# Newton's values partly in PSUM, held weight sums and an unsplit half of h in a two-layer fp32 step

## The chip, the cores and the metric

One Trainium2 chip, one of its cores. The metric is the device time of one launch in microseconds (us); smaller is better. TensorE does the matrix products; VectorE (DVE), ScalarE (ACT) and GpSimd (POOL) do the rest, each with its own in-order queue; SyncE (SP) issues nearly all DMAs, in a fixed list.

## The reference

One inference step of a two-layer model, all in fp32: 640 tokens (512 latent, 128 prompt), width 1024, feed-forward width 2816.

```python
every layer: x += 1/2 * gate1 * SwiGLU1(mod(rmsnorm(x)))
             x += gate2 * Mixer_l(mod(rmsnorm(x)))
             x += 1/2 * gate3 * SwiGLU2(mod(rmsnorm(x)))
mod(h) = h * (1 + scale) + shift

def rms_norm(x, g):
    y = x * rsqrt(mean(x * x, axis=-1) + EPS)
    return y * g
def swiglu(h, w_gate, w_up, w_down):
    return (silu(h @ w_gate) * (h @ w_up)) @ w_down
```

Layer 0's mixer is neighbourhood attention beside a bidirectional linear recurrence; layer 1's is a 2-D Fourier transform with a linear map. Shift, scale and gate come from a conditioning vector. Latent and prompt tokens have different ones.

## The kernel before, in words

The activations lie transposed: 1024 features are 8 chunks `c` of 128 partitions, and the 640 tokens are two halves `h` (0 and 1) of `HT` = 320 columns. An fp32 product is three products of rounded parts: each operand is split into a high and a low tile, and `mm3` (line 282) issues high by high, high by low and low by high. So each weight tile `st` that a DMA brings is split into `whi` (ACT, line 176) and `wlo` (DVE, line 181), and each chunk of the normed activations `h` into `hh` and `hl`.

The four SwiGLUs are the stages 0ffn1, 0ffn2, 1ffn1 and 1ffn2. Layer 0's mixer lies between the first two, layer 1's between the last two. Of the 22 blocks `f` of 128 hidden features the first two are made directly, from four weight tiles: the fill of `ffn_body`, a loop over half `h` and chunk number `n`, with product `j` inside. The rest are made by `quad`, a scheme of seven block products M1 to M7 in place of eight. It needs

- sums of weight blocks, made on POOL by `quad_b` (lines 226, 227) and `quad_c` (lines 231, 232) out of a gate tile and an up tile, and then split by ACT and DVE (`quad_a`, `quad_d`, `quad_e`, `quad_f`);
- the T factors, sums over the halves of h, tiles `T[0..3][k]`, `k` = 0 to 3. `t_sums` (line 528) makes them from the chunks `k` and `k+4` of both halves while half 1 is normed, in three steps; line 172 is the low part of their split.

`prep` takes the next steps of a list of weight work: it issues loads (`load`), the DVE low parts still due (`flush`) and one or more of the steps above. It is called at j = 3 of every `n`, so weight work and norm work stand in one order on each engine. A load is issued when a buffer `st` is free, and a split when a pair `whi`/`wlo` is free; both are kept in lists with a phase, and `buffers` adds some for one stage.

The norm of a half: the sums of squares come from TensorE into a bank `nst`; `rsqrt` (lines 415 to 422) takes the inverse root by three Newton steps of three small DVE operations (128 x 3 each), with `nv`, `nt` and `ns` in SBUF; the result is spread by a matmul to the bank `nbc`; then `norm_high` and `norm_low` make each chunk: line 473 multiplies x by `nbc`, ACT lines 479 and 481 apply scale and shift and take the high part, and line 495 makes the low part (on POOL for even chunks of half 0). For odd chunks of half 0 (`direct`) one DVE operation (line 469), one of ACT (line 471) and one of DVE (line 492) do the same. Tiles `y` rotate through three buffers. Half 0 of the next stage is normed inside the last product of the stage before, chunk by chunk after the update of x (line 381); half 1 inside the fill's h = 0 (start) and h = 1.

The scratch PSUM bank has room beside the few columns that `nst` uses. In `t_sums` half 0 is only there split, so the factors that need it take the high part, and then the low part in an operation of its own:

## Time and profile before

| | us |
|---|---|
| median of 3 runs (lowest, highest) | 2299.74 (2299.42, 2300.52) |
| profiled execution, its own time | 2300.82 |
| its span in the profile | 2299.0 |
| TensorE busy in the span | 2223.4 |
| DVE busy | 1550.3 |
| ACT busy | 990.1 |
| POOL busy | 953.6 |

The profiled execution's own time is 1.8 us longer than its span, and 1.1 us above the median. Stages by time in the span: 0ffn1 to about 515 us, layer 0's mixer to about 835, 0ffn2 to about 1305, 1ffn1 to about 1770, layer 1's mixer to about 1855, 1ffn2 to the end. In a timeline row the columns are: start, length of one group, engine, line, operation, output from inputs, shapes, count, and in square brackets the idle time of the engine ahead of it with what ended it. In a table of stretches each row is one stretch: its length, then each engine's busy time with its number of instructions, the granted TensorE clock as a share of the full one, the share of the DMA engines' time, and GB/s.

### The profile page before, as it was taken

The page shows a single profiled execution, that of the slowest core. Times are in us where ns is not written, and L with a number is a line of the kernel's source. Part 1 is how long each engine was busy: PE and PEld are TensorE (multiplying, and loading weights), DVE is VectorE, ACT ScalarE, POOL GpSimd, SP SyncE. Part 2 cuts the span into 40 slices and gives each one's busy share as a digit, 9 for nine tenths or more (in the row PEclk, how much of TensorE's full clock was granted, in tenths as well). Part 3 has the DMA queues.
Part 4 walks back from the last instruction along what each step waited for, and adds up shares of the span by engine and source line. Part 5 has one row for each costly group of instructions (what it writes and reads, how often), then busy time and mean ns, then how long its engine had stood idle before and what let it go on. Part 6 is the DMA issues. An engine that isn't in the chain of part 4 may idle for free.

```text
span 2299.0 us, 39900 instructions
## 1 busy us (share of the span) xinstructions
PE 2223.4 (97%) x15534; PEld 2111.4 (92%) x15534; DVE 1550.3 (67%) x2871; ACT 990.1 (43%) x1780; POOL 953.6 (41%) x856
## 2 busy tenths in 40 slices
PE   6899999999998899999999999999999989999999
PEld 5899999999995798999999989999999979999999
DVE  6676676666865368666666786666667786666665
ACT  4433333347765444333333453333335553333332
POOL 2544444440023235444444454444443645444441
PEclk9999999999999999999999999999999999999999
DMA  7333333321228424322332143332232322222221
GB/s 279 113 108 104 110 104 111 106 83 56 67 74 272 130 96 144 108 94 102 111 106 85 67 156 123 107 110 93 101 111 62 129 91 78 83 83 83 83 90 56
DMA packets 75317, 245.44 MB, mean 107 GB/s; under 512 B 8757, under 2 KB 12997, under 8 KB 75129
## 3 DMA queue, kind: packets, MB, share of 16 engines
q1 hardware_dynamic: 74168, 241.28, 31.0%
q8 instruction: 123, 2.02, 0.4%
q10 hardware_dynamic: 864, 1.38, 0.2%
q14 instruction: 66, 0.53, 0.1%
q0 software_dynamic: 96, 0.22, 0.0%
HBM read 239.71 MB, written 3.15 MB: 106 GB/s over the span
## 4 chain that ended last, share of the span: by engine, by line
PE 78%; DVE 12%; ACT 4%; issue 2%; POOL 2%; DMA 2%; DVEq 0%; SPq 0%; ACTq 0%; POOLq 0%
PE q L282 39%; PE pd L282 27%; PE pj L282 5%; DVE wlo L181 2%; PE ada L327 2%; DVE tl L172 1%; DMA st<-w_ada 1%; PE gt L1014 1%; PE pg L282 1%; PE pos L1549 1%; DVE x L381 1%; ACT hh L481 1%; DVE y L473 1%; DVE hl L495 0%; POOL u L825 0%
## 5 line engine op out<-in xcount | busy, mean ns | idle before, releaser
L181 DVE TENSOR_TENSOR wlo<-st,whi 128x1024 fp32r<-128x1024 f32 (+2 forms) x401 | 496.3, 1248 | 11.9 <-ACT whi L176 11.0
L176 ACT ACTIVATE whi<-st 128x1024 fp32r<-128x1024 f32 (+2 forms) x405 | 401.2, 992 | 235.2 <-POOL st L232 143.5
L282 PE MATMUL pd<-g,whi 128*128 128x320 f32 x1536 | 347.6, 311 | 2.7 <-DVE u L825 2.0
L381 DVE SCALAR_TENSOR_TENSOR x<-pd,mods,x 128x128 f32<-128x128 f32 (+2 forms) x696 | 265.1, 431 | 113.7 <-PE pd L282 113.5
L282 PE MATMUL q<-hh,wlo 128*128 128x320 f32 x960 | 297.0, 309 | 5.6 <-DVE wlo L181 5.6
L282 PE MATMUL q<-hh,whi 128*128 128x320 f32 x960 | 300.9, 313 | 0.6 <-DVE u L825 0.5
L282 PE MATMUL q<-th,whi 128*128 128x320 f32 x960 | 297.9, 310 | 3.0 <-DVE sg L825 3.0
L282 PE MATMUL q<-tl,whi 128*128 128x320 f32 x960 | 297.3, 310 | 0.7 <-POOL tl L172 0.7
L282 PE MATMUL q<-th,wlo 128*128 128x320 f32 x960 | 297.1, 310 | 0.0
L282 PE MATMUL q<-hl,whi 128*128 128x320 f32 x960 | 296.4, 309 | 0.0
L231 POOL TENSOR_TENSOR st<-sums,st 128x512 f32<-128x512 f32 x80 | 117.9, 1474 | 399.6 <-DVE wlo L181 362.2
L825 POOL TENSOR_TENSOR u<-u,u 128x320 f32<-128x320 f32 x80 | 107.4, 1343 | 402.0 <-DVE u L825 402.0
L282 PEld LDWEIGHTS pd<-g,whi 128*128 128x128 f32 x1536 | 257.6, 188 | 6.8 <-issue 2.9
L282 PE MATMUL pd<-hh,whi 128*128 128x320 f32 x768 | 238.7, 311 | 0.0
L282 PE MATMUL pd<-hl,whi 128*128 128x320 f32 x768 | 238.2, 310 | 0.0
L282 PE MATMUL pd<-g,wlo 128*128 128x320 f32 x768 | 238.1, 310 | 0.0
L282 PE MATMUL pd<-hh,wlo 128*128 128x320 f32 x768 | 237.2, 309 | 0.0
L826 ACT ACTIVATE sg<-sg 128x320 f32<-128x320 f32 x160 | 75.4, 471 | 284.2 <-DVE sg L825 284.2
L282 PEld LDWEIGHTS q<-hh,whi 128*128 128x128 f32 x960 | 180.4, 188 | 16.3 <-issue 8.6
L282 PEld LDWEIGHTS q<-th,whi 128*128 128x128 f32 x960 | 180.8, 188 | 6.3 <-issue 5.1
L282 PEld LDWEIGHTS q<-hh,wlo 128*128 128x128 f32 x960 | 180.2, 188 | 6.7 <-DVE wlo L181 6.7
L282 PEld LDWEIGHTS q<-tl,whi 128*128 128x128 f32 x960 | 181.0, 189 | 1.5 <-POOL tl L172 1.5
(327 smaller groups left out, 5006.9 us busy)
## 6 DMA issues: line engine op xcount, KB each, us to landing
st<-w_ada SPq DMA_DIRECT2D x144, 512.0 KB, 4.5
st<-ffn_gate SPq DMA_DIRECT2D x88, 512.0 KB, 3.5
st<-ffn_up SPq DMA_DIRECT2D x88, 512.0 KB, 3.6
st<-ffn_down SPq DMA_DIRECT2D x96, 384.0 KB, 3.0
st<-w_in SPq DMA_DIRECT2D x20, 512.0 KB, 3.5
st<-ffn_down SPq DMA_DIRECT2D x16, 512.0 KB, 3.5
st<-w_out_ab SPq DMA_DIRECT2D x8, 512.0 KB, 3.6
st<-w_out_c SPq DMA_DIRECT2D x8, 512.0 KB, 3.5
```

The lines of the kernel that those rows point to most:

```text
L172: (eng or self.nc.vector).tensor_tensor(out=lo, in0=src, in1=hi.bitcast(F32), op=ALU.subtract)
L176: self.nc.scalar.activation(out=hi, in_=src, func=AF.Copy)
L181: self.low.tensor_tensor(out=lo, in0=src, in1=hi.bitcast(F32), op=ALU.subtract)
L231: self.nc.gpsimd.tensor_tensor(out=s[:, 0:512], in0=it.s1, in1=s[:, 0:512], op=ALU.subtract)
L282: self.nc.tensor.matmul(out, lhsT=l, rhs=r, start=first and j == 0, stop=last and j == len(ops) - 1)
L327: nc.tensor.matmul(self.ada_ps[32 * j:32 * j + 32, 0:256], lhsT=self.s_sb[:, k, :], rhs=t[:, 256 * j:256 * j + 256], start=k == 0, stop=k ...
L381: self.nc.vector.scalar_tensor_tensor(out=self.x[h][c][:, sl], in0=ps[:, sl], scalar=gate[:, c, r:r + 1], in1=self.x[h][c][:, sl], op0=ALU ...
L473: nc.vector.tensor_tensor(out=y, in0=self.x[h][c], in1=r, op=ALU.mult)
L481: nc.scalar.activation(out=hi, in_=y, func=AF.Copy)
L825: tt = lambda e, o, a, b, op=ALU.add: e.tensor_tensor(out=o, in0=a, in1=b, op=op)
L826: cp = lambda o, p, fn=AF.Copy: nc.scalar.activation(out=o, in_=p, func=fn)
L1014: nc.tensor.matmul(g[:, s, 0:322], lhsT=wt[:, d, j, :], rhs=xc[:, 322 * s:322 * s + 322], start=True, stop=True)
```

## The change

1. In `rsqrt`, `v` and `t_` lie in columns 4 to 8 and 8 to 12 of the PSUM bank that holds the sums of squares, and the products are ordered so that each of the 11 operations has an operand there. Their number stays.
2. Where the four T factors' pool is made whole (ahead of 0ffn2, 1ffn1 and 1ffn2, not 0ffn1), it gets eight tiles `raw0`. Half 0 of the normed activations stays there unsplit; `t_sums` reads it, and drops two POOL operations for each `k`, 24 in all. `direct` is off there, so 12 odd chunks take lines 473, 479, 481 and 495.
3. 0ffn1 gets one more raw weight buffer and one more `whi`/`wlo` pair.
4. In the fill of 0ffn2 and 1ffn1, the first four `n` of h = 0 only load and flush. The weight steps that stood there (the sums of quad f = 2) come at n = 4 to 6.
5. Two small parameter loads go through ACT's queue and not POOL's, and the scratch space for POOL's DMA descriptors is set to 1024 bytes.

```diff
 def rsqrt(self, ps, n=3):
-        v, s, t_ = (self.t2.tile([P, 3], F32, tag=t, name=t)[:, :n] for t in ("nv", "ns", "nt"))
+        v, s, t_ = (x[:, :n] for x in (ps[:, 4:8], self.t2.tile([P, 3], F32, tag="ns", name="ns"), ps[:, 8:12]))
...
-            nc.vector.tensor_tensor(out=t_, in0=s, in1=s, op=ALU.mult)
-            nc.vector.scalar_tensor_tensor(out=t_, in0=t_, scalar=-0.5, in1=v, op0=ALU.mult, op1=ALU.mult)
+            nc.vector.tensor_tensor(out=t_, in0=v, in1=s, op=ALU.mult)
+            nc.vector.scalar_tensor_tensor(out=t_, in0=t_, scalar=-0.5, in1=s, op0=ALU.mult, op1=ALU.mult)
 def T_pool(self, ks=range(4)):
+        self.raw0 = [tp.tile([P, HT], F32, name=f"r{c}") for c in range(KD)] if len(ks) == 4 else None
 def norm_high(self, h, l, i, c, r, keep):
+        elif keep and not h and self.raw0:
+            y = self.raw0[c]
 def direct(self, l, i, h, c, keep):
-        return h == 0 and c % 2 == 1
+        return h == 0 and c % 2 == 1 and not (keep and self.raw0)
 def t_sums(self, k, b12, b22):
+        if self.raw0:
+            b11, b21 = self.raw0[k], self.raw0[k + 4]
...
-        tt(self.T_ENG[0], b12, b12, l11)
+        if not self.raw0:
+            tt(self.T_ENG[0], b12, b12, l11)
...
-        tt(nc.gpsimd, t4, t4, l21, ALU.add)
+        if not self.raw0:
+            tt(nc.gpsimd, t4, t4, l21, ALU.add)
 def ffn(...):
-            self.buffers(gp, ph, 3, 0)
+            self.buffers(gp, ph, *((4, 1) if ph == "0ffn1" else (3, 0)))
 def ffn_body(...):
-                    if j == 3:
+                    if j == 3 and h == 0 and n < 4 and (l, i) != (1, 2):
+                        self.flush()
+                        self.load()
+                    elif j == 3:
                         self.prep(self.n_use + 1, 1)
...
-            nc.gpsimd.dma_start(out=pk, in_=a["pk"])
+            nc.scalar.dma_start(out=pk, in_=a["pk"])
...
-    nc = _bacc.Bacc("TRN2", target_bir_lowering=False, num_devices=1)
+    nc = _bacc.Bacc("TRN2", target_bir_lowering=False, num_devices=1, dynamic_dma_scratch_size=1024)
```

The change moves instructions at three places. First, DVE at the start of 1ffn1, from the last chunk of half 0's norm to the Newton steps of half 1 (`st_`, `wlo_` and `whi_` are weight buffers by number, `hl_102` and `hh_101` chunk 7 of h, `r_7855` its unsplit tile). Before:

```order
L469 SCALAR_TENSOR_TENSOR y<-x_85,sc,nbc 128x320
L492 SCALAR_TENSOR_TENSOR hl_102<-y,mods,hh_101 128x320
L181 TENSOR_TENSOR wlo_76<-st_66,whi_75 128x1024
L181 TENSOR_TENSOR wlo_68<-st_65,whi_67 128x1024
L415 TENSOR_SCALAR nv<-nst 128x3
L417 TENSOR_SCALAR ns<-nv 128x3
L420 TENSOR_TENSOR nt<-ns 128x3
L421 SCALAR_TENSOR_TENSOR nt<-nt,nv 128x3
```

The same place in the change:

```order
L477 TENSOR_TENSOR r_7855<-x_85,nbc 128x320
L499 TENSOR_TENSOR hl_102<-r_7855,hh_101 128x320
L181 TENSOR_TENSOR wlo_74<-st_64,whi_73 128x1024
L415 TENSOR_SCALAR nst<-nst 128x3
L417 TENSOR_SCALAR ns<-nst 128x3
L420 TENSOR_TENSOR nst<-nst,ns 128x3
L421 SCALAR_TENSOR_TENSOR nst<-nst,ns 128x3
```

Of the two weight splits ahead of the Newton steps one is left. The other stands later on DVE, in the norm of half 1 (`b_13218` is chunk 0 of half 1, `pg` and `sg` belong to the SwiGLU of block 0); 0ffn2 has both moves too:

```order
L499 TENSOR_TENSOR hl_96<-y,hh_95 128x320
L534 TENSOR_TENSOR b_13218<-b_13218,r_7848 128x320
L181 TENSOR_TENSOR wlo_76<-st_66,whi_75 128x1024
L737 TENSOR_TENSOR sg<-sg,pg 128x320
L172 TENSOR_TENSOR g_13122<-sg,g_13121 128x320
```

Second, POOL at the start of 0ffn2, from the low parts of half 0 through the weight sums to the T factors of k = 0 and 1 (`t_` and `b_` are factors being made, `tl_` their low parts). Before:

```order
L495 TENSOR_TENSOR hl_100<-y,hh_99 128x320
L226 TENSOR_TENSOR sums<-st_65 128x512
L227 TENSOR_TENSOR st_65<-st_66,st_65 128x512
L231 TENSOR_TENSOR st_66<-sums,st_66 128x512
L232 TENSOR_TENSOR st_66<-st_66 128x512
L528 TENSOR_TENSOR t_8576<-y,b_8559 128x320
L528 TENSOR_TENSOR b_8559<-b_8559,hl_88 128x320
L528 TENSOR_TENSOR t_8638<-hh_95,y 128x320
L528 TENSOR_TENSOR t_8638<-t_8638,hl_96 128x320
L172 TENSOR_TENSOR tl_7870<-t_8576,th_7869 128x320
L528 TENSOR_TENSOR t_8656<-y,b_8570 128x320
```

In the change:

```order
L499 TENSOR_TENSOR hl_100<-r_7854,hh_99 128x320
L534 TENSOR_TENSOR t_8565<-y,b_8548 128x320
L226 TENSOR_TENSOR sums<-st_66 128x512
L227 TENSOR_TENSOR st_66<-st_64,st_66 128x512
L231 TENSOR_TENSOR st_64<-sums,st_64 128x512
L232 TENSOR_TENSOR st_64<-st_64 128x512
L534 TENSOR_TENSOR t_8632<-r_7852,y 128x320
L172 TENSOR_TENSOR tl_7873<-t_8565,th_7872 128x320
L534 TENSOR_TENSOR t_8649<-y,b_8559 128x320
```

The four sums go behind the first T operation, and each k has three POOL operations in place of five.

Third, DVE near the end of 0ffn1, where its last product updates x and half 0 is normed for the mixer (`x_86` is half 1 of x, `hl_90` chunk 1). Before:

```order
L473 TENSOR_TENSOR y<-x_85,nbc 128x320
L492 SCALAR_TENSOR_TENSOR hl_90<-y,mods,hh_89 128x320
L181 TENSOR_TENSOR wlo_68<-st_64,whi_67 128x1024
L381 SCALAR_TENSOR_TENSOR x_86<-pd,mods,x_86 128x192
L381 SCALAR_TENSOR_TENSOR x_86<-pd,mods,x_86 128x128
```

In the change:

```order
L477 TENSOR_TENSOR y<-x_85,nbc 128x320
L496 SCALAR_TENSOR_TENSOR hl_90<-y,mods,hh_89 128x320
L381 SCALAR_TENSOR_TENSOR x_86<-pd,mods,x_86 128x192
L381 SCALAR_TENSOR_TENSOR x_86<-pd,mods,x_86 128x128
```

One weight split of three among these updates has left the place; it now stands ahead of the earlier weight work, where the buffer pair added in 0ffn1 is free.

## The prediction, on record before the change was run

> **What bounds the kernel now.** I read the page's busy times first, then the table of stretches, then TensorE's timeline at the stretches that lose time, then DVE's and POOL's timelines there.

> ```profile
> PE 2223.4 (97%) x15534; PEld 2111.4 (92%) x15534; DVE 1550.3 (67%) x2871; ACT 990.1 (43%) x1780; POOL 953.6 (41%) x856
> ```

> TensorE bounds the kernel, and the change leaves its instructions alone. Only time that TensorE loses can be won. The table says where that is.

> ```profile
> 60.00:120.00 60.00, 52.32 (x370) 47.64 (x369) 40.27 (x68) 26.28 (x51) 30.60 (x26) 0.97 0.34 119
> 500.00:535.00 35.00, 30.41 (x199) 28.88 (x200) 30.07 (x76) 22.38 (x41) 12.53 (x30) 1.00 0.21 69
> 835.00:930.00 95.00, 88.27 (x605) 81.61 (x605) 78.95 (x134) 42.63 (x79) 51.15 (x45) 0.96 0.38 134
> 930.00:1270.00 340.00, 340.00 (x2360) 331.55 (x2359) 217.47 (x355) 131.38 (x218) 148.26 (x119) 1.00 0.30 100
> 1300.00:1400.00 100.00, 94.47 (x669) 86.20 (x668) 79.35 (x136) 43.77 (x83) 51.93 (x46) 0.98 0.40 138
> 1850.00:1912.00 62.00, 56.03 (x360) 51.90 (x361) 52.42 (x89) 32.12 (x65) 37.30 (x35) 0.94 0.25 85
> ```

> From 930 to 1270 TensorE has no gap: 340 us for 2360 matmuls, 0.144 us each. By that pitch the starts of the stages lose 60 - 370 x 0.144 = 6.7 us (0ffn1), 35 - 199 x 0.144 = 6.3 (its end), 7.9 (0ffn2), 3.7 (1ffn1) and 10.2 (1ffn2), some 35 us. The change works at these five places and nearly nowhere else. The losses are single waits of TensorE:

> ```profile
> 76.12 0.41 PE L282 MATMUL pg<-hh,whi 128*128 128x320 f32 x1 [4.44 <-ACT hh L481]
> 120.06 0.56 PE L282 MATMUL pd<-g,whi 128*128 128x320 f32 x2 [1.99 <-DVE u L825]
> 514.94 0.38 PE L282 MATMUL pj<-hh,whi 128*128 128x320 f32 x1 [2.54 <-ACT hh L471]
> 881.93 0.41 PE L282 MATMUL q<-hh,wlo 128*128 128x320 f32 x1 [1.65 <-DVE wlo L181]
> 898.58 0.39 PE L282 MATMUL q<-th,whi 128*128 128x320 f32 x1 [1.09 <-DVE sg L825]
> 1307.88 0.42 PE L282 MATMUL pg<-hh,wlo 128*128 128x320 f32 x1 [2.60 <-DVE wlo L181]
> 1881.65 0.41 PE L282 MATMUL pg<-hl,whi 128*128 128x320 f32 x1 [1.74 <-DVE hl L495]
> 1909.69 0.55 PE L282 MATMUL q<-th,whi 128*128 128x320 f32 x1 [1.88 <-DVE sg L825]
> ```

> and behind the longer ones, slices in which the granted clock is half:

> ```profile
> 121.20:124.60 3.40, 3.40 (x15) 3.40 (x14) 3.27 (x10) 2.40 (x3) 0.00 (x0) 0.50 0.56 212
> 1309.00:1312.40 3.40, 3.40 (x15) 3.40 (x14) 3.12 (x9) 0.00 (x0) 2.55 (x2) 0.50 0.93 335
> 1909.80:1913.20 3.40, 3.40 (x13) 3.40 (x14) 2.04 (x6) 1.86 (x4) 0.06 (x1) 0.51 0.47 161
> ```

> Such a slice does 13 to 15 matmuls where the dense pitch does 24. It costs (24 - 15) x 0.144 = 1.3 us by the count and 3.4 / 2 = 1.7 by the clock; I take 1.5. Slices stand behind the gaps of 1.99, 2.60 and 1.88 us; the gaps of 1.74 and 1.65 had none. So a gap that shrinks below about 1.8 us should win 1.5 us on top.

> **The change, part by part.**

> *Newton in PSUM.* In 0ffn2 the Newton steps of half 1 run while POOL makes weight sums:

> ```profile
> 842.69 0.15 DVE L415 TENSOR_SCALAR nv<-nst 128x3 f32<-128x3 f32 x1
> 842.87 1.05 DVE L417 TENSOR_SCALAR ns<-nv 128x3 int32<-128x3 int32 x1
> 848.47 0.16 DVE L422 SCALAR_TENSOR_TENSOR ns<-nt,ns 128x3 f32<-128x3 f32 x1
> 850.18 0.49 DVE L473 TENSOR_TENSOR b<-x,nbc 128x320 f32<-128x320 f32 x1 [0.75 <-PE nbc L453]
> 841.79 2.10 POOL L226 TENSOR_TENSOR sums<-st 128x512 f32<-128x512 f32 x1 [1.65 <-DMA st<-ffn_up]
> 887.36 0.47 DVE L729 TENSOR_TENSOR sg<-sg,pg 128x320 f32<-128x320 f32 x1
> 887.05 1.54 POOL L226 TENSOR_TENSOR sums<-st 128x512 f32<-128x512 f32 x1
> ```

> Line 417, all in SBUF, takes 1.05 us under POOL's line 226; the same kind takes 0.16 without it. Line 415, which reads PSUM, takes 0.15 under it, and line 729, which reads PSUM, 0.47 in the middle of another sum. So an operation with a PSUM operand does not wait for POOL. Four of the 11 operations are long here, about 4 x 0.9 = 3.6 us of DVE time. TensorE has the fill's h = 0 to do meanwhile, and waits only for the end of it: I count 0.7 us in 0ffn2 (the wait at nbc), and set the same in 1ffn2 against the longer ACT work below. A write to PSUM by a small DVE operation is nowhere in this trace; the bounds are 0.16 us (no cost) and 1.05 us (as bad as a delayed one), and I take 0.16, by the nearer row, line 415, which has one side in PSUM. With 11 x 0.9 us at the six norms on the path the upper bound would be 60 us, but most of that would be covered as the 3.6 us are now.

> [...]

> *Held sums.* In 1ffn1 half 0's first matmuls wait for weight splits that stand two in a row on DVE; one of the two splits a weight for the later quad:

> ```profile
> 1305.54 3.41 DVE L181 TENSOR_TENSOR wlo<-st,whi 128x1024 fp32r<-128x1024 f32 x2
> 860.20 0.89 POOL L528 TENSOR_TENSOR t<-hh,y 128x320 f32<-128x320 f32 x1 [5.20 <-DVE y L528]
> ```

> Without it, and without the four sums that slow DVE there, the gap of 2.60 shrinks by about half of 3.41, 1.7 us, and falls below 1.8: -1.7 - 1.5 = -3.2 us. The bounds are 0 (another wait takes its place) and -2.6 - 1.5 = -4.1. The held sums cost POOL 6.3 us (2.1 + 3 x 1.4, by the first and the 887.05 row's length) and land behind the first T operation, where POOL now idles 5.2 us; the remaining 1 us comes back from the dropped operations. If the cover is gone, the T factor of k = 0 is late by about 1 us.

> *Unsplit half 0.* The norm of half 1 sets the pace in the fill's h = 1:

> ```profile
> 865.24 0.47 DVE L473 TENSOR_TENSOR y<-x,nbc 128x320 f32<-128x320 f32 x1
> 869.36 1.16 DVE L495 TENSOR_TENSOR hl<-y,hh 128x320 fp32r<-128x320 f32 x1
> 872.34 0.47 DVE L473 TENSOR_TENSOR y<-x,nbc 128x320 f32<-128x320 f32 x1
> 868.27 1.02 POOL L528 TENSOR_TENSOR t<-t,hl 128x320 f32<-128x320 f32 x1
> 1303.68 0.56 ACT L471 ACTIVATE hh<-y,mods 128x320 fp32r<-128x320 f32 x1 [0.61 <-DVE y L469]
> 1855.65 1.07 DVE L417 TENSOR_SCALAR ns<-nv 128x3 int32<-128x3 int32 x1
> 1856.96 1.14 DVE L421 SCALAR_TENSOR_TENSOR nt<-nt,nv 128x3 f32<-128x3 f32 x1
> 1848.07 0.65 ACT L479 ACTIVATE y<-y,mods,sc 128x320 f32<-128x320 f32 x1 [5.60 <-DVE y L473]
> 1848.76 0.47 ACT L481 ACTIVATE hh<-y 128x320 fp32r<-128x320 f32 x1
> ```

> A pair of chunks takes 872.34 - 865.24 = 7.10 us of DVE; TensorE needs 24 matmuls x 0.144 = 3.5 us and the weight work between. Each of the dropped POOL operations lasts 1.0 us and stretches one DVE operation beside it by up to 1.16 - 0.48 = 0.7. Two fewer per pair give 1.4 us at most and I take 0.8. Over the two or three pairs that bind this closes the gap of 1.74 (1ffn2: -1.7) and half of 1.65 (0ffn2: -0.8); the T chain behind is one POOL operation shorter, which closes 1.09 (0ffn2: -1.0) and 1.0 of 1.88 (1ffn2: -1.0, and half a slice, -0.8). Against it ACT does 0.65 + 0.47 - 0.56 = 0.56 us more per odd chunk, 2.2 us per stage. In 0ffn2 and 1ffn1 this lies beside DVE's x updates; in 1ffn2 the norm of half 0 is on the path, and the 2.2 us are partly met by Newton, where the two long operations at 1855.65 and 1856.96 lose 1.9: +0.3 by the difference, and I take +0.8 since ACT's work comes first. DVE's part stays: two operations for two.

> *The extra buffers in 0ffn1.*

> ```profile
> 95.42 1.29 POOL L226 TENSOR_TENSOR sums<-st 128x512 f32<-128x512 f32 x1 [9.85 <-DMA st<-ffn_up]
> 72.76 1.54 DVE L473 TENSOR_TENSOR y<-x,acc 128x320 f32<-128x320 f32 x1
> 66.21 0.49 DVE L473 TENSOR_TENSOR b<-x,acc 128x320 f32<-128x320 f32 x1
> 511.27 1.90 DVE L181 TENSOR_TENSOR wlo<-st,whi 128x1024 fp32r<-128x1024 f32 x1
> ```

> POOL waits 9.85 us for a tile that no free buffer let in earlier. With one more it starts sooner, the chain of the first quads is earlier, and the gap of 1.99 with its slice goes: -3.5 us. But the sums move up beside the norm of half 1, where a DVE operation takes 1.54 for 0.49, and I add 1.5 to the gap of 4.44. Net -2.0; bounds +3 (two more stretched operations and no gap closed) and -5.6. At the stage's end one split fewer stands among the x updates, of 1.90 us; the wait of 2.54 loses 1.8, bounds 0 and -2.5.

> *The two parameter loads and the scratch space* lie at the very start. No row prices them; I set 0, and -0.5 to +0.5 as bounds, about one small operation (0.55) won on POOL's queue or lost on ACT's.

> **The sum.** 0ffn1 start -2.0, its end -1.8; 0ffn2 -0.7 - 0.8 - 1.0 and -0.7 for its smaller gaps = -3.2; 1ffn1 -3.2; 1ffn2 -1.7 - 1.8 + 0.8 = -2.7. Together -12.9. On the profiled execution 2300.8 - 12.9 = 2287.9; that execution stands 1.1 above the median, so I forecast **2287 us**. Less than 0.2%, 4.6 us either way, is about what a measurement cannot tell from no change.

> **The rivals.**

> *Half gains.* The waits move on to the next engine: in 1ffn1 the wait for wlo becomes one for its `whi`, and the 4.44 of 0ffn1 grows as much as the later gap shrinks. Then only the terms that a shorter queue gives outright remain, -1.8 at 0ffn1's end and -1.0 twice: 2296, within 0.2%. For it speaks that five engines meet at these places; against it that ACT is busy 43% and POOL 41%.

> *The slices stay.* The half clock may come at fixed moments behind any start of a stage. Then -1.5 twice and -0.8 are lost: 2291. The three slices behind gaps of 1.88 or more and none behind 1.74 speak against it. [...]

> *Slower.* The held sums and their split land in the T stretch of 0ffn2 and 1ffn1, which DVE paces. One split (1.9 stretched) and four sums, each stretching a DVE operation by 0.7, make 1.9 + 2.8 = 4.7 us per stage more on DVE; less 3 pairs x 0.8 won leaves +2.3, and a gap above 1.8 brings a slice of 1.5: +3.8 twice, with +3 in 0ffn1: 2310. It decides if DVE's pair stays at 7.1 us and the sums do not fit POOL's idle 5.2.

> *PSUM is dear.* If a small PSUM write costs as much as a delayed SBUF operation, 1.05, Newton grows by 7 x 0.9 = 6 us on DVE where 4 of 11 are long now, some 2 us of it seen at four of the starts: 2287 + 8 = 2295.

> **Chances.** The forecast 0.55, slices stay 0.15, half gains 0.13, PSUM dear 0.07, slower 0.10. The range holds the first three and PSUM's price on the upper side, to 2297; on the lower, the far ends of the terms (0ffn1 -5.6 and -2.5, 1ffn1 -4.1, and -6 and -5 for 0ffn2 and 1ffn2 if the pair wins 1.4 in place of 0.8 and their small gaps close) make -23, 2277. Faster by over 0.2% (under 2295): 0.76; within: 0.15; slower: 0.09.

> **What would show it.** Newton's operations all at 0.15 to 0.2 us beside POOL's sums; a pair at about 6.3 us; no gap of 1.7 or more at 881, 1307 and 1881; full clock behind them; POOL's wait of 9.85 gone and TensorE's wait near 76 at 4.4 to 6; x updates near 513 one split earlier. The prediction is wrong if the gaps reappear behind `sg`, `hl` or `hh` in the same stretches, or if the T stretch of 0ffn2 ends later than before, counted from the stage's start.

## The result, and the profile after

The change takes 2286.3 us (median of 6 runs, 2285.29 to 2291.68), the kernel before 2300.82 (median of 6, 2299.42 to 2302.80): ratio 0.994, 95% interval 0.9928 to 0.9952. That is 14.5 us less; 2287 was forecast, from terms that sum to 12.9 us less. The profiled execution has a span of 2283.8 us, 15.2 shorter than before's 2299.0. The direction and the total came out; the parts did not all come out, and one assumption behind the sum was wrong.

The page's busy times: the count of matmuls is the same, POOL has 26 operations fewer (the 24 of the T factors and two DMA issues) and ACT 12 more.

```profile
PE 2217.3 (97%) x15534; PEld 2104.6 (92%) x15534; DVE 1540.5 (67%) x2871; ACT 993.5 (44%) x1792; POOL 948.9 (42%) x830
```

The table of stretches, with the starts and ends moved to the same places of the program (the first row has the same times as before):

```profile
60.00:120.00 60.00, 54.92 (x396) 50.26 (x396) 46.30 (x81) 27.77 (x53) 31.77 (x26) 1.00 0.40 133
495.00:530.00 35.00, 31.16 (x205) 29.36 (x204) 29.25 (x80) 21.43 (x40) 12.67 (x30) 1.00 0.17 54
829.00:919.40 90.40, 85.42 (x605) 78.50 (x605) 73.20 (x134) 43.80 (x81) 43.64 (x36) 1.00 0.41 140
1290.50:1386.80 96.30, 93.01 (x667) 84.81 (x668) 74.74 (x136) 44.72 (x85) 44.78 (x37) 1.00 0.43 144
1836.80:1895.40 58.60, 53.98 (x362) 50.09 (x362) 46.55 (x87) 33.27 (x69) 30.44 (x26) 0.98 0.25 84
```

In 60 us TensorE does 396 matmuls for 370; the stretch of 605 matmuls in 0ffn2 takes 90.4 us for 95.0. The clock column stands at 1.00 in four of the five, where it had 0.97, 1.00, 0.96, 0.98 and 0.94.

Since both kernels issue the same 15534 matmuls in the same order, the start of each can be compared with the start of the same one before. By this the profiled executions, one launch each, differ as follows (good to a few tenths, since some records can be missing):

| place (time before) | measured, us | forecast |
|---|---|---|
| 0ffn1, start (0 to 128) | -5.8 | -2.0 (with the next row) |
| 0ffn1, middle (128 to 490) | +1.7 | |
| 0ffn1, end (490 to 535) | -0.9 | -1.8 |
| layer 0's mixer (535 to 830) | -0.9 | 0 |
| 0ffn2, start (830 to 930) | -4.5 | -3.2 |
| 930 to 1290 | +0.4 | 0 |
| 1ffn1, start (1290 to 1400) | -3.0 | -3.2 |
| 1400 to 1853 | -0.3 | 0 |
| 1ffn2, start (1853 to 1930) | -2.3 | -2.7 |
| 1930 to the end | +0.8 | 0 |

TensorE's waits of the change, from its timeline:

```profile
69.11 0.42 PE L282 MATMUL pg<-hh,whi 128*128 128x320 f32 x1 [1.59 <-ACT hh L485]
75.31 0.42 PE L282 MATMUL pg<-hh,whi 128*128 128x320 f32 x1 [2.35 <-ACT hh L485]
130.37 0.56 PE L282 MATMUL pd<-g,whi 128*128 128x320 f32 x2 [1.22 <-DVE x L381]
509.84 0.38 PE L282 MATMUL pj<-hh,whi 128*128 128x320 f32 x1 [1.63 <-ACT hh L475]
830.77 0.41 PE L282 MATMUL pg<-hh,wlo 128*128 128x320 f32 x1 [1.71 <-DVE wlo L181]
1297.13 0.41 PE L282 MATMUL pg<-hh,wlo 128*128 128x320 f32 x1 [1.05 <-DVE wlo L181]
1847.22 1.05 PE L455 MATMUL nbc<-dg,ones 128*128 128x128 f32 x6 [1.20 <-DVE dg L430]
1867.51 0.42 PE L282 MATMUL pg<-hl,whi 128*128 128x320 f32 x1 [0.86 <-DVE hl L499]
1878.05 0.42 PE L282 MATMUL q<-hh,wlo 128*128 128x320 f32 x1 [0.94 <-DVE wlo L181]
1893.85 0.39 PE L282 MATMUL q<-th,whi 128*128 128x320 f32 x1 [1.51 <-DVE sg L836]
```

One wait of before at these places, and the two half-clock slices behind it, do not stand in the prediction's lists:

```profile
837.03 0.41 PE L282 MATMUL pg<-hh,wlo 128*128 128x320 f32 x1 [1.90 <-DVE wlo L181]
838.00:844.80 6.80, 6.80 (x30) 6.80 (x29) 5.88 (x9) 2.57 (x5) 3.79 (x3) 0.50 0.55 172
```

4.44 became 2.35, 2.54 became 1.63, 1.90 became 1.71, 2.60 became 1.05, 1.74 became 0.86 and 1.88 (near 1909) 1.51; those near 120, 881 and 898 are under a microsecond. New are 1.59 us near 69, 1.22 near 130 and 1.20 at `nbc` in 1ffn2. So of the 2.1 us that the wait of 4.44 lost, 1.6 stand in the new wait ahead of it. The clock's slices behind the waits are gone in this launch; one is left in layer 0's mixer (at 768) and three in a row at the end of layer 1's:

```profile
831.00:834.40 3.40, 3.40 (x27) 3.40 (x27) 1.90 (x6) 3.27 (x7) 0.87 (x1) 1.00 0.50 159
1297.20:1300.60 3.40, 3.40 (x23) 3.40 (x24) 2.40 (x13) 0.00 (x0) 0.00 (x0) 1.00 0.69 234
1829.20:1832.60 3.40, 3.28 (x16) 3.22 (x16) 2.57 (x14) 0.00 (x0) 0.00 (x0) 0.50 0.01 2
```

Half of the time at half clock, summed over the span, is 17.2 us before and 7.2 in the change: 10 of the 15 us. The profiled launch of the change has the highest granted clock of its six (0.997; the others 0.992 to 0.996), and the launches of before in all experiments have 0.988 to 0.993. So part of these 10 us belongs to this launch.

### The profile page after: what moved, and what is told of

It reads as the page before. It is cut to its first block, busy times and chain, and to the rows that moved or that the text cites. A ratio compares the mean times of both kernels' runs of the same rounds, so it can differ in the third digit from the quotient of the medians.

```text
span 2283.8 us, 39869 instructions
## 1 busy us (share of the span) xinstructions
PE 2217.3 (97%) x15534; PEld 2104.6 (92%) x15534; DVE 1540.5 (67%) x2871; ACT 993.5 (44%) x1792; POOL 948.9 (42%) x830
## 4 chain that ended last, share of the span: by engine, by line
PE 78%; DVE 11%; ACT 5%; issue 2%; POOL 1%; DMA 1%; ACTq 0%; DVEq 0%; SPq 0%; POOLq 0%
PE q L282 40%; PE pd L282 26%; PE pj L282 5%; DVE wlo L181 2%; PE ada L327 2%; DVE tl L172 1%; DMA st<-w_ada 1%; DVE hl L499 1%; ACT hh L485 1%; PE gt L1025 1%; PE pos L1560 1%; DVE x L381 1%; ACT sx L1282 0%; DVE y L477 0%; ACT r L483 0%
## 5 line engine op out<-in xcount | busy, mean ns | idle before, releaser
L181 DVE TENSOR_TENSOR wlo<-st,whi 128x1024 fp32r<-128x1024 f32 (+2 forms) x401 | 499.8, 1257 | 16.2 <-ACT whi L176 15.6
L282 PE MATMUL pd<-g,whi 128*128 128x320 f32 x1536 | 347.6, 311 | 2.0 <-DVE x L381 1.9
L282 PE MATMUL q<-hh,whi 128*128 128x320 f32 x960 | 301.0, 314 | 1.0 <-DVE u L836 1.0
L282 PE MATMUL q<-hh,wlo 128*128 128x320 f32 x960 | 297.1, 310 | 2.9 <-DVE wlo L181 2.9
L282 PE MATMUL q<-th,whi 128*128 128x320 f32 x960 | 297.4, 310 | 2.2 <-DVE sg L836 2.2
L282 PE MATMUL q<-th,wlo 128*128 128x320 f32 x960 | 296.8, 309 | 0.0
L282 PE MATMUL q<-hl,whi 128*128 128x320 f32 x960 | 296.5, 309 | 0.0
L282 PE MATMUL q<-tl,whi 128*128 128x320 f32 x960 | 296.4, 309 | 0.0
L231 POOL TENSOR_TENSOR st<-sums,st 128x512 f32<-128x512 f32 x80 | 125.0, 1563 | 367.8 <-DVE wlo L181 353.8
L282 PEld LDWEIGHTS pd<-g,whi 128*128 128x128 f32 x1536 | 256.9, 188 | 6.9 <-issue 3.3
L282 PE MATMUL pd<-hh,whi 128*128 128x320 f32 x768 | 239.8, 312 | 0.0
L282 PE MATMUL pd<-hl,whi 128*128 128x320 f32 x768 | 238.5, 311 | 0.0
L282 PE MATMUL pd<-hh,wlo 128*128 128x320 f32 x768 | 238.2, 310 | 0.0
L282 PE MATMUL pd<-g,wlo 128*128 128x320 f32 x768 | 237.1, 309 | 0.0
L282 PEld LDWEIGHTS q<-hh,whi 128*128 128x128 f32 x960 | 180.4, 188 | 16.7 <-issue 9.9
L282 PEld LDWEIGHTS q<-th,whi 128*128 128x128 f32 x960 | 180.4, 188 | 5.6 <-issue 3.5
L282 PEld LDWEIGHTS q<-hh,wlo 128*128 128x128 f32 x960 | 180.3, 188 | 3.7 <-DVE wlo L181 3.7
L282 PEld LDWEIGHTS q<-th,wlo 128*128 128x128 f32 x960 | 180.7, 188 | 0.0
```

The lines of the kernel that those rows point to most:

```text
L181: self.low.tensor_tensor(out=lo, in0=src, in1=hi.bitcast(F32), op=ALU.subtract)
L231: self.nc.gpsimd.tensor_tensor(out=s[:, 0:512], in0=it.s1, in1=s[:, 0:512], op=ALU.subtract)
L282: self.nc.tensor.matmul(out, lhsT=l, rhs=r, start=first and j == 0, stop=last and j == len(ops) - 1)
```

## The experiments

The theory to test (A): each part shortens its own waits of TensorE, the half-clock slices go with the waits, and the parts add. The rival (B): the gain belongs to the clock alone, and the parts overlap. Part 5 (the parameter loads and the scratch space) was not run by itself; it is in the runs of the unsplit half alone and of the buffers alone. Ratios below are to the kernel before, on the same chip, with 95% intervals; 0.001 is 2.3 us.

### Each part alone

**Newton alone.** The diff is part 1 of the change, against before:

```diff
-        v, s, t_ = (self.t2.tile([P, 3], F32, tag=t, name=t)[:, :n] for t in ("nv", "ns", "nt"))
+        v, s, t_ = (x[:, :n] for x in (ps[:, 4:8], self.t2.tile([P, 3], F32, tag="ns", name="ns"), ps[:, 8:12]))
```

> Part 1 alone (Newton's v and t_ in PSUM), all else as before. Theory A (the parts add: each shortens its own waits of TensorE, and the half-clock slices go with the waits that it shortens): all 11 operations of a Newton at 0.15 to 0.2 us also beside POOL's sums, DVE some 3.6 us less in 0ffn2; -1 to -3 us, since TensorE waits only for the last part of it. Theory B (the gain is one of the clock and the parts overlap: a slice goes only when several parts together bring a wait under about 1.85 us): -1 or less. Theory C (PSUM writes are dear): the operations take 0.25 us or more, 0 to +4 us.

Measured: 0.9973 (0.9962 to 0.9983), 6.2 us faster, over twice what theory A gave. The operations are as expected. The groups by line over the 12 Newtons, before first, then this kernel (the last number ahead of the second bar is the mean length in ns):

```profile
L421 DVE SCALAR_TENSOR_TENSOR nt<-nt,nv 128x3 f32<-128x3 f32 (+1 forms) x36 | 8.3, 231 | 1.2
L417 DVE TENSOR_SCALAR ns<-nv 128x3 int32<-128x3 int32 (+1 forms) x12 | 4.4, 371 | 0.4
```

```profile
L421 DVE SCALAR_TENSOR_TENSOR nst<-nst,ns 128x3 f32<-128x3 f32 (+1 forms) x36 | 6.1, 170 | 1.2
L417 DVE TENSOR_SCALAR ns<-nst 128x3 int32<-128x3 int32 (+1 forms) x12 | 1.9, 160 | 0.4
```

170 ns with both sides in PSUM, where the same line took 160 to 170 in SBUF with POOL idle (823.55 and 824.73 in before): the write there costs 0.01 us at most, and theory C is out. All five lines together go from 31.8 us to 21.9. Over half of the gain in kernel time is seen in 0ffn2. Half 0's Newton, before the stage, has one long operation in before (line 417), beside POOL's sum of squares (line 393), and none here; then TensorE's first wait in the stage, and the stretch behind it:

```profile
822.52 0.80 DVE L417 TENSOR_SCALAR ns<-nv 128x3 int32<-128x3 int32 x1
822.41 0.88 POOL L393 TENSOR_TENSOR acc<-acc,sq 128x320 f32<-128x320 f32 x1 [6.22 <-ACT sq L391]
```

```profile
820.06 0.16 DVE L417 TENSOR_SCALAR ns<-nst 128x3 int32<-128x3 int32 x1
833.99 0.41 PE L282 MATMUL pg<-hh,wlo 128*128 128x320 f32 x1 [1.32 <-DVE wlo L181]
837.00:840.40 3.40, 3.40 (x23) 3.16 (x23) 3.30 (x7) 0.57 (x1) 1.79 (x2) 1.00 0.24 61
```

0.64 us less on DVE shortens the wait from 1.90 to 1.32, the clock stays full, and TensorE is 3.5 us earlier between 830 and 846. Of the 5.4 us that this profile is ahead of before's, 3.5 arise there; another 2.9 lie in layer 0's mixer, where before's slice at 698 is missing. That this slice is Newton's is not shown: two runs with Newton's values in SBUF (the unsplit half alone, and the idle matmuls in before) lack it too.

**Unsplit half alone.** Part 2 of the change, with part 5, against before; the line that sets it:

```diff
+        self.raw0 = [tp.tile([P, HT], F32, name=f"r{c}") for c in range(KD)] if len(ks) == 4 else None
```

> Part 2 alone (half 0 kept unsplit for the T factors; with the smaller descriptor scratch, all else as before). Theory A: a pair of chunks in the fill's h = 1 at about 6.3 us for 7.1; TensorE's waits at 881 and 1881 gone and those at 898 and 1909 about 1 us less; -4 to -6 us, in 0ffn2, 1ffn1 and 1ffn2. Theory B: the pair is shorter, but TensorE's waits pass to the next weight split; -1 to -3.

Measured: 0.9979 (0.9968 to 0.9990), 4.8 us faster, as theory A said. A pair of chunks in 0ffn2 on DVE:

```profile
859.13 0.48 DVE L477 TENSOR_TENSOR y<-x,nbc 128x320 f32<-128x320 f32 x1
865.38 0.48 DVE L477 TENSOR_TENSOR y<-x,nbc 128x320 f32<-128x320 f32 x1
```

6.25 us, where before had 7.10. The stretch from 846 to 930 is 2.3 us shorter than before's, that from 1853 to 1930 1.5, the one from 1290 to 1400 1.2. The waits at 881 and 1881 fall to 0.76 and 0.87 us, as theory A said; those at 898 and 1909 fall by 0.3 and not by 1. One wait grows: the first of 0ffn2 is 2.28 us for 1.90. There DVE's low part (line 499) takes 1.13 us for 0.85 and the split that TensorE waits for 1.58 for 1.40, both beside POOL's low parts.

**Held sums alone.** Part 4, against before:

```diff
+                    if j == 3 and h == 0 and n < 4 and (l, i) != (1, 2):
+                        self.flush()
+                        self.load()
+                    elif j == 3:
-                    if j == 3:
```

> Part 4 alone (the sums of quad f = 2 held until n = 4 to 6 in 0ffn2 and 1ffn1). Theory A: the wait of 2.60 at 1307 is down to 0.9 or so and the half clock behind it is gone; in 0ffn2 the Newton steps are free of POOL's sums without part 1; -3 to -5 us. Theory B: without part 2, POOL's T chain is late by the held sums (about 6 us of POOL against 5.2 idle), the waits at 881 and 898 grow; -2 to +3.

Measured: 0.9992 (0.9984 to 1.0001), not to be told from no change. Both theories are half right, as TensorE's timeline shows for 1ffn1 and 0ffn2:

```profile
1309.13 0.41 PE L282 MATMUL pg<-hh,wlo 128*128 128x320 f32 x1 [0.75 <-DVE wlo L181]
1336.26 0.41 PE L282 MATMUL pg<-hl,whi 128*128 128x320 f32 x1 [1.73 <-DVE hl L499]
```

```profile
840.45 0.50 PE L282 MATMUL pg<-hh,wlo 128*128 128x320 f32 x1 [1.90 <-DVE wlo L181]
873.55 0.42 PE L282 MATMUL pg<-hl,whi 128*128 128x320 f32 x1 [1.73 <-DVE hl L499]
```

In 1ffn1 the wait of 2.60 is down to 0.75 (-3.4 us up to 1313), and 1.7 of it is given back in the T stretch, where a wait of 1.73 for `hl` is new. In 0ffn2 the first wait stays at 1.90 and the later one grows (+1.3 us from 846 to 930). That is the rival "slower" of the prediction, for a part by itself. (The profiled launch is the longest of its eleven; it has three half-clock slices in a row at 516, 3.8 us, where before has none.)

**Buffers alone.** Part 3, with part 5, against before:

```diff
-            self.buffers(gp, ph, 3, 0)
+            self.buffers(gp, ph, *((4, 1) if ph == "0ffn1" else (3, 0)))
```

> Part 3 alone (0ffn1 with one more raw buffer and one more pair; with the smaller descriptor scratch and the parameter loads on ACT's queue). Theory A: all of what 0ffn1 gains comes from here, -4 us up to its middle and -1 at its end as in the trace of the change; -4 to -6. Theory B: the gain in 0ffn1 is the two half-clock slices (behind the waits at 76 and 120) and hangs on where the waits fall; -2 to -4 on the median, with profiles in which a slice is back.

Measured: 0.9983 (0.9974 to 0.9993), 3.9 us faster, between the theories. Its profile is 4.2 us ahead between 60 and 128, gives 1.8 back up to 490 and wins 0.9 at the stage's end. The slice near 120 is gone, but two stand behind the wait near 76, where the change's profile has none; of the six runs with these buffers and no idle matmuls, only the change's has none between 71 and 77. To that extent theory B is right: these slices hang on the launch. The wait that 0ffn1 gets back, near 130, is for an update of x; in the change, DVE shows why:

```profile
126.39 3.46 DVE L181 TENSOR_TENSOR wlo<-st,whi 128x1024 fp32r<-128x1024 f32 x2 [1.57 <-ACT whi L176]
```

The pair of buffers that was added lets two weight splits run ahead; beside POOL's sums (lines 226 and 227, from 125.22 to 128.77) they take 1.7 us each, where the one at 66.36, with POOL idle, takes 1.2, and the update that TensorE waits for stands behind them in DVE's queue.

### Each part left out

The same four edits, each undone in the change.

Without Newton in PSUM:

> The change without part 1: Newton's values all in SBUF again. Theory A: 1 to 3 us slower than the change (ratio to before 0.9945 to 0.9955 where the change has 0.994), lost in 1ffn2, where POOL makes sums beside Newton; in 0ffn2 and 1ffn1 the held sums already leave POOL free there. Theory B: some 0 to 1. Theory C (PSUM dear): faster than the change.

Measured: 0.9953 (0.9939 to 0.9966), 3 us slower than the change's 0.994. Not where theory A put it: between 830 and 846 it has lost all, 3.2 us, since the long operation of half 0's Newton is back (0.80 us), and what runs beside it is POOL's sum of squares, which no part of the change moves. TensorE's first wait in 0ffn2 and the stretch behind it:

```profile
834.56 0.41 PE L282 MATMUL pg<-hh,wlo 128*128 128x320 f32 x1 [2.28 <-DVE wlo L181]
836.90:843.70 6.80, 6.80 (x32) 6.80 (x33) 4.05 (x16) 1.76 (x3) 0.74 (x1) 0.58 0.52 184
```

2.28 us for 1.71, and nearly two slices at half clock. So at this wait Newton in PSUM takes off about 0.57 us (1.90 to 1.32, and 2.28 to 1.71 beside the unsplit half) and the unsplit half adds about 0.38. In 1ffn2 0.8 us are lost.

Without the unsplit half:

> The change without part 2. Theory A: 4 to 6 us slower than the change (ratio about 0.996): the pair of chunks back at 7.1 us, waits back at 881, 898, 1881 and 1909. Theory B: more than what it gains alone, 6 to 9, since the held sums now meet the longer T chain on POOL and waits over 1.85 us bring slices.

Measured: 0.9954 (0.9940 to 0.9968), 3.2 us slower than the change; theory A's place, B's cause: the wait of 1.72 for `hl` stands in both stages where sums are held, as with held sums alone, and 846 to 930 is 2.7 us longer than in the change, 1313 to 1400 3.0.

Without held sums:

> The change without part 4. Theory A: 3 to 5 us slower than the change: the wait near 1307 back at 2.0 to 2.6 with a half-clock slice, one us in 0ffn2. Theory B: 0 to 2, since the unsplit half and the PSUM operands already take the stretch out of the waits.

Measured: 0.9945 (0.9932 to 0.9958), 1.2 us slower than the change, within the intervals. In its profile the wait near 1307 is 2.26 us, with two slices, of which the first begins ahead of the wait, and 846 to 930 is 1.0 us shorter than in the change. That this us is the hold's is not shown: the run below that holds in 1ffn1 alone has the same program in 0ffn2 and is no shorter there than the change.

Without the buffers:

> The change without part 3. Theory A: 4 to 6 us slower than the change, all in 0ffn1, with the waits at 76 and 120 and their slices as before. Theory B: 2 to 4.

Measured: 0.9958 (0.9942 to 0.9974), 4.1 us slower than the change. The wait at 74 is 4.43 us again, and a slice stands behind it and one near 120.

Together (us, from the ratios; each alone is good to about 2.5 us, each difference to about 4):

| part | alone | left out of the change |
|---|---|---|
| Newton in PSUM | -6.2 | +3.0 |
| unsplit half | -4.8 | +3.2 |
| held sums | -1.8 | +1.2 |
| buffers in 0ffn1 | -3.9 | +4.1 |
| sum | -16.7 | +11.5 |
| all four | -13.8 | |

Within their errors the parts add, but these errors are wide: none of the four kernels with a part left out differs from the change by more than its error. Theory B in its strict form is out: two parts alone bring 5 and 6 us.

### The clock by itself

Idle matmuls are put ahead of a wait, so that TensorE is busy there; no work is taken away. The edit, at three places in before and at six in the change:

```diff
+    def spin(self, n):
+        if n:
+            p = self.bank("spin")[:, 0:HT]
+            for _ in range(n):
+                self.nc.tensor.matmul(p, lhsT=self.wz[:, 0:P], rhs=self.wz, start=True, stop=True)
```

> The kernel before (with the smaller descriptor scratch, for room), and three groups of idle matmuls (128x320 on a tile of ones, into a bank that nothing reads) that TensorE runs just ahead of three of its waits: 16 ahead of the wait of 4.44 us at 76, 8 each ahead of those at 837 and 1307. No wait ends sooner by them and no work is taken away. Theory A (a half-clock slice follows any of the fixed 3.41 us windows in which TensorE is idle for 1.8 us or more): the waits of TensorE there shrink to 2.0, 0.7 and 1.4 us, the slices behind them (1.7, 3.4 and 1.7 us lost in the profile of before) are gone, and the kernel is 3 to 6 us faster than before by doing more work. Theory B (the slices come with the start of a stage, or after a count of work): they stay; 0, or slower by up to 1 us.

Measured: 1.0003 (0.9995 to 1.0012): no gain. The three waits shrink as theory A said, to 1.96, 0.72 and 1.47 us, but the slices go behind two of them only; one stays behind the wait near 76. Three stretches behind waits that were filled or met next, and TensorE's and DVE's rows of the second:

```profile
835.80:839.20 3.40, 3.40 (x28) 3.40 (x27) 2.58 (x5) 2.90 (x5) 1.30 (x2) 1.00 0.48 154
846.10:849.50 3.40, 2.27 (x8) 1.93 (x9) 1.78 (x8) 0.00 (x0) 0.00 (x0) 0.50 0.17 70
1308.60:1312.00 3.40, 3.40 (x25) 3.29 (x23) 3.26 (x6) 0.00 (x0) 2.48 (x2) 1.00 0.80 270
```

```profile
847.23 1.84 PE L461 MATMUL nbc<-dg,ones 128*128 128x128 f32 x6 [3.47 <-DVE dg L438]
842.10 1.08 DVE L425 TENSOR_SCALAR ns<-nv 128x3 int32<-128x3 int32 x1
843.40 1.12 DVE L429 SCALAR_TENSOR_TENSOR nt<-nt,nv 128x3 f32<-128x3 f32 x1
```

The slices behind 837 and 1307 are gone, and TensorE is 2.9 us earlier at 846. There it waits 3.47 us for `nbc`, behind DVE's stretched Newton, and that wait brings two slices of its own: 5.1 us lost again by 930. In 1ffn1 TensorE is 1.5 us earlier at 1313, waits 1.52 us for `nbc`, where before had no wait, and has lost 1.2 again by 1400. So a full clock alone is worth nothing there. DVE's chain is as late as TensorE's, and only the part that shortens DVE makes the clock count.

> The change, with idle matmuls ahead of TensorE's waits that are left in it: 6 and 10 in 0ffn1 (at 69 and 75), 5 in 0ffn2 (at 830), and 8, 12 and 10 in the norm at the end of layer 1's mixer (1826 to 1836), where it had three slices in a row of half clock. Theory A: the slices at 1829 are gone, which brings the norm's matmuls and the first of 1ffn2 to full clock; 2 to 5 us faster than the change (ratio to before 0.992 to 0.993). Theory B: no difference, or slower by 1 to 2 where a group runs past the end of its wait.

Measured: 0.9932 (0.9918 to 0.9945), not to be told from the change. The same thing happens at the end of layer 1's mixer: the slices at 1829 are gone, and TensorE waits 2.43 us for the next `nbc` (1.20 in the change), with two slices.

```profile
1829.90:1833.30 3.40, 3.40 (x28) 3.40 (x28) 2.62 (x15) 0.00 (x0) 0.00 (x0) 1.00 0.01 2
1847.52 1.81 PE L468 MATMUL nbc<-dg,ones 128*128 128x128 f32 x6 [2.43 <-DVE dg L441]
```

### Holding in one stage, and both edits

```diff
-                    if j == 3 and h == 0 and n < 4 and (l, i) != (1, 2):
+                    if j == 3 and h == 0 and n < 4 and (l, i) == (1, 0):
```

> The change with the sums held in 1ffn1 alone, no longer in 0ffn2. Theory A (from the four single parts: holding gains 2 to 3.4 us at the start of 1ffn1 and costs 1.0 to 1.3 in 0ffn2 between 846 and 930): 0.5 to 1.5 us faster than the change, in 0ffn2 alone. Theory B: in 0ffn2 POOL's sums are back beside the norm of half 1 and the wait near 837 is over 1.8 us again, with a slice: 0 to 3 us slower.

Measured: 0.9940 (0.9927 to 0.9952), the ratio of the change. The stretch in 0ffn2 is no shorter than in the change (-2.83 and -1.59 against -2.84 and -1.66), and its first wait is 1.73 us without a slice behind it, so neither theory is borne out: beside the new T chain no cost of holding in 0ffn2 is seen here.

> The idle matmuls of the last but one run and the sums held in 1ffn1 alone, in one kernel. If both theories A hold, 3 to 6 us faster than the change, ratio to before 0.9915 to 0.9927.

Measured: 0.9955 (0.9943 to 0.9967), 3.5 us slower than the change. In its profile one slice each stands at 70, 692, 842, 1296 and 1852, where the change's profile has none; at the end of the mixer 12 idle matmuls ran at half clock, 3.55 us, and the next matmuls follow them without a wait, so they ran past the wait that they were to fill. No version here beats the change by more than the intervals.

## Why the prediction was right, and where it was not

**Where time is lost.** Right: -15 us, of which -17 at the five starts and ends named and +2 given back between them. The T stretch of 0ffn2 (846 to 930) is 1.7 us shorter and not longer. Of the gaps that I named as signs of being wrong, the one behind `sg` near 1909 is still 1.51 us, and one behind `hh` is new in 0ffn1.

**Newton.** The operations came out exactly (0.16 to 0.17 us, the lower bound). The term was mis-sized: "TensorE waits only for the end of it: I count 0.7 us in 0ffn2", and the same in 1ffn2. Alone it is 6.2 us, left out 3.0. The step that failed is that I priced half 1's Newton, where four operations are long, and not half 0's, where one is (822.52, 0.80 us). That one lies on the path to the first wait of 0ffn2, which with its two slices was missing from my lists; its 0.64 us take that wait from 1.90 to 1.32, with no slice behind it, and 3.5 us are won by 846. For the other 2.7 of the 6.2 no cause is shown. In 1ffn2 the term was 0.7; the stretch won 0.2 alone and lost 0.8 where the part was left out.

**Unsplit half.** Pair 7.10 to 6.25 us (0.85; 0.8 assumed). Its terms, -0.8, -1.0, -1.7, -1.0, -0.8 and +0.8, make -4.5; alone it is -4.8. The 1ffn2 stretch came to -2.3 for -2.7. I put ACT's longer work beside DVE's x updates in 0ffn2 and let it cost nothing there; the first wait of 0ffn2 is 0.38 us longer by this part. In 1ffn2, where I took +0.8, the change waits 1.20 us at `nbc` (1.29 with this part alone) where before had no wait, and DVE's idle times ahead of that end with ACT's `hh`.

**Held sums.** -3.2 was forecast for 1ffn1 and 1ffn1's start has -3.0, but that is the work of two parts: alone the hold gains 3.4 there and gives 1.7 back, since the held sums stretch DVE's operations in the T stretch (in 0ffn2 of the change a line 534 at 844.96 takes 1.58 us beside POOL's line 227, and 0.48 at 856.68 with POOL idle). The cover that I named, the dropped POOL operations, was needed; the rival's mechanism is real and the unsplit half is what keeps it off. The bound of "0 (another wait takes its place)" was the better value for the part by itself.

**Buffers.** Net -4.1 in 0ffn1's start and middle, for -2.0; with the end, -5.0 for -3.8, and 3.9 or 4.1 by the timed runs. POOL's wait of 9.85 us is down to 2.46, and two sums moved up beside the norm of half 1, as I said (72.44 and 74.03 in before, 63.32 and 64.68 in the change, where a line 473 takes 1.54 us for 0.55). But the wait of 4.44, which I had let grow by 1.5, shrank to 2.35, and a new one of 1.59 stands ahead of it: a weight split went ahead too, on DVE from 69.03 to 66.36. The two waits together are 3.94. What was given back is elsewhere, the wait near 130 for an update of x that I had not seen.

**The slices.** I let a slice be worth 1.5 us on top of its wait, and counted 3.8 us in all. The slices behind 4.44 and 1.90 were not counted, and the limit of about 1.8 us passed over the wait of 2.54, which had none. In the two profiles 10 us less are lost to the half clock. But the idle matmuls show that the price does not hold by itself: 2.9 us won there were lost at the next wait. The sum came out because the waits and the slices went together, with DVE's chain shortened beside them, and because terms that were too small (Newton, the start of 0ffn1) met one that was too large (the held sums) and a loss of 1.7 us after the start of 0ffn1 that no term had; that was luck as far as the argument went. Of the rivals, "the slices stay" and "PSUM is dear" are shown wrong; "half gains" and "slower" did not come about for the whole, though the hold alone shows the second.

## What to carry to other kernels

Small DVE operations that were long beside POOL's SBUF work (0.80 to 1.15 us) took 0.16 to 0.17 us here with an operand in PSUM, no more than in SBUF with POOL idle (0.16 to 0.17, from 823.35 to 824.93 in before); look for such operations on the path to a wait, also where only one of them is long. A wait that another engine ends is priced with what follows: here shortening the chain that ends it brought TensorE's clock along (1.90 to 1.32 us, and 3.5 us won by 846), while filling TensorE with idle work only moved the wait (2.9 us won by 846, 5.1 lost again by 930). Work that is put off needs its cover shown in the same kernel; here one part is worth something only beside another.
